# Exp of the last four rows taken row by row in a kernel that sums reciprocals

## The chip, the cores and the metric

One core of a Trainium2 chip. The metric is the device time of one execution in microseconds (us). Engines are named as the profile names them: PE (TensorE), DVE (VectorE), ACT (ScalarE), POOL (GpSimd), SP (SyncE).

## The reference

```python
x = np.abs(np.random.randn(32, 512, 1024)).astype(np.float32) + 1e-6
out = np.sum(1.0 / x, axis=-1)      # 32 x 512 float32
```

Each of the 128 partitions gets 128 rows of 1024 elements: 67 MB to read, 64 KB to write.

## The kernel before

A row is folded in half: 1/a + 1/b = (a + b) / (ab). With the product p = ab, the reciprocal is exp(-ln p), which ACT makes with one Ln and one Exp on half as many elements. There are three kinds of chunk, of two rows each:

- **A**: POOL makes both products. Exp writes the reciprocals rc to PSUM, and DVE sums the whole row (1024 elements) times rc: 1.2 us per row.
- **B**: POOL makes both products. PE adds the halves (a matmul with the identity, accumulated) into s in PSUM; Exp is in place in pr; DVE sums 512 elements of pr times s: 0.68 us per row.
- **C**: like B, but the product of the first row is made by DVE from a copy b of the half row that PE puts into PSUM.

```python
A, B, C = (2, 0, 0), (2, 2, 0), (2, 2, 1)          # rows, rows summed through s, rows whose product DVE makes
LOADS = [[A, B, A, B], [A, B, A, C]] * 5 + [[A, B], [A, C]] * 4 + [[A], [B], [A], [C]] * 2
...
def sum_rows(c, xc, pr, sm, rc):
    m, e = xc.shape[1], len(sm)
    for j in range(e, m):                           # rows of kind A
        row = xc[:, j, :].rearrange("p (h e) -> p h e", h=2)
        sum_row(c + j, row,
                rc[:, j - e, :].unsqueeze(1).to_broadcast([P, 2, H]),
                pr[:, e : e + 2, :] if j == e and m - e > 1 else None)   # where the products go; None: over the row
    for j in reversed(range(e)):                    # rows of kinds B and C, the second one first
        sum_row(c + j, pr[:, j, :], sm[j])
...
        for (m, e, v), pr in zip(chunks, made):     # one chunk
            xc = xt[:, q : q + m, :]
            ...                                     # POOL: products of rows v..m-1 into pr
            sm = []
            for j in range(e):                      # PE: s of row 0, then s of row 1
                s = spool.tile([P, H], f32, tag="s")
                add(s, xc[:, j, :H], xc[:, j, H:])
                sm.append(s)
            if waiting:
                sum_rows(*waiting)                  # DVE: sums of the chunk before
            keep(nc.scalar.activation(out=pr, in_=pr, func=Ln, scale=S))
            rc = None
            if e < m:                               # kind A: one Exp of both rows
                rc = rpool.tile([P, m - e, H], f32, tag="rc")      # rpool has 2 buffers
                i = nc.scalar.activation(out=rc, in_=pr[:, e:, :], func=Exp, scale=-1.0)
                keep(i)
            if e:                                   # kinds B, C: one Exp of both rows
                r = pr[:, :e, :]
                keep(nc.scalar.activation(out=r, in_=r, func=Exp, scale=-1.0))
            waiting = c0 + q, xc, pr, sm, rc
```

The order on every engine is that of the program. The last two chunks are an A (rows 124, 125) and a C (rows 126, 127), each loaded by itself.

## Time and profile before

| | before |
|---|---|
| time, median of 3 | 171.85 us (171.72 to 171.97) |
| span in the profile | 169.9 us |
| PE starts on the last load | 161.10 us |
| last sum's accumulator read starts | 167.06 us |

The last two rows: I call the stretch between them **the tail** (5.96 us here) and what follows to the end of the span **the end phase** (169.94 - 167.06 = 2.88 us: the store and the final barrier). The accumulator read is the instruction that writes a row's finished sum out. Measuring the tail from PE's start takes out the jitter of the loads, which is some tenths of a us. The lines themselves are in the prediction. In a timeline a line has the start and the length in us, the engine, the line of the kernel and the operation, what is written and read, shapes, the count, and in brackets how long the engine had been idle and what released it. L92 is the summing helper on DVE; its form over 1024 elements (ANT_1) is a row of kind A, that over 512 (ANT_0) a row of kind B or C.

### The profile page before, as it was taken

How to read it: one execution, taken by the hardware profiler on the slowest of the kernel's cores; microseconds unless marked ns; L12 is line 12 of the kernel's file. 1: busy time of each engine (PE TensorE's matmuls, PEld its weight loads, DVE VectorE, ACT ScalarE, POOL GpSimd, SP SyncE). 2: the span in 40 equal slices, each digit the busy share in tenths (PEclk: the TensorE clock that was granted, in tenths of full speed). 3: DMA queues.
4: the chain of work that ended last, by engine and by line, in shares of the span. 5: the costliest groups of instructions: out<-in, count | busy, mean ns of one | idle time of the engine just before them, and what ended most of it. 6: DMA issues, size and time to landing. Idle time of an engine off the chain costs nothing.

```text
span 169.9 us, 1267 instructions
## 1 busy us (share of the span) xinstructions
PE 131.7 (77%) x278; PEld 50.5 (30%) x278; DVE 122.3 (72%) x267; ACT 133.9 (79%) x129; POOL 138.3 (81%) x70
## 2 busy tenths in 40 slices
PE   0008999786988789784997869789999999888790
PEld 0003433331332233231432323224334342333230
DVE  0000777767987577767777679778989898889883
ACT  3002989978887987958889787999999988999890
POOL 1008999699996999689996998999999889998920
PEclk9999999999999999999999999999999999999999
DMA  6999999999999999999999999999999999999400
GB/s 208 409 455 409 463 409 455 409 463 401 463 411 447 424 440 420 432 434 424 440 424 440 424 397 434 424 428 426 432 428 432 424 413 417 422 420 424 187 0 15
DMA packets 3894, 67.24 MB, mean 396 GB/s; under 512 B 432, under 2 KB 560, under 8 KB 560
## 3 DMA queue, kind: packets, MB, share of 16 engines
q1 hardware_dynamic: 3888, 67.18, 92.9%
q8 instruction: 2, 0.03, 0.1%
q14 instruction: 4, 0.03, 0.0%
HBM read 67.11 MB, written 0.07 MB: 395 GB/s over the span
## 4 chain that ended last, share of the span: by engine, by line
DMA 78%; POOL 11%; DVE 3%; ACT 2%; issue 2%; SPq 1%; POOLq 0%; DVEq 0%
DMA ring<-in_x_dram 78%; POOL pr L141 11%; DVE pr L92 2%; DVE ring L92 1%; ACT pr L152 1%; ACT rc L156 1%; SPq L122 1%; POOLq L141 0%; DVE sums L92 0%; DVEq L92 0%; DVEq L195 0%
## 5 line engine op out<-in xcount | busy, mean ns | idle before, releaser
L141 POOL TENSOR_TENSOR pr<-ring 128x1024 f32<-128x1024 f32 x64 | 137.6, 2189 | 23.6 <-DMA ring<-in_x_dram 23.3
L82 PE MATMUL s<-ring,ident 128*128 128x512 f32 x256 | 122.4, 616 | 32.5 <-DVE sums L92 16.6
L152 ACT ACTIVATE pr<-pr 128x1024 f32<-128x1024 f32 x64 | 67.4, 1053 | 28.7 <-POOL pr L141 28.5
L82 PEld LDWEIGHTS s<-ring,ident 128*128 128x128 f32 x256 | 47.0, 194 | 105.3 <-issue 63.1
L92 DVE CUSTOM_DVE_ANT_1 pr<-ring,rc 128x1024 f32<-128x1024 f32 x32 | 39.1, 1221 | 44.6 <-ACT rc L156 44.6
L92 DVE CUSTOM_DVE_ANT_0 pr<-pr,s 128x512 f32<-128x512 f32 x64 | 41.3, 683 | 0.2
L92 DVE CUSTOM_DVE_ANT_1 ring<-ring,rc 128x1024 f32<-128x1024 f32 x32 | 38.9, 1216 | 0.0
L162 ACT ACTIVATE pr<-pr 128x1024 f32<-128x1024 f32 x32 | 33.8, 1058 | 1.0
L156 ACT ACTIVATE rc<-pr 128x1024 f32<-128x1024 f32 x32 | 32.9, 1028 | 1.0
L82 PE MATMUL b<-ring,ident 128*128 128x512 f32 x22 | 12.0, 626 | 1.4 <-DMA ring<-in_x_dram 1.4
L92 DVE DVE_READ_ACCUMULATOR2_ANT sums<- 128x1 f32 x128 | 10.6, 83 | 0.0
L130 DVE TENSOR_TENSOR pr<-ring,b 128x512 f32<-128x512 f32 x11 | 7.5, 683 | 0.1
L82 PEld LDWEIGHTS b<-ring,ident 128*128 128x128 f32 x22 | 3.5, 188 | 9.0 <-DMA ring<-in_x_dram 7.6
L53 ACT ACT_TABLE_LOAD x1 | 1.3, 1283 | 0.7 <-PEq L184 0.7
masks.py:197 POOL MEMSET ident<- 128x128 f32 x1 | 0.2, 204 | 0.3 <-POOLq L184 0.3
masks.py:199 POOL TENSOR_SCALAR_AFFINE_SELECT ident<-ident 128x128 f32<-128x128 f32 x1 | 0.3, 292 | 0.1
L184 POOL MEMSET const-float32-0.0<- 128x1 f32 x1 | 0.1, 98 | 0.2 <-issue 0.2
L184 POOL MEMSET const-uint8-127<- 128x1 uint8 x1 | 0.1, 103 | 0.0
L184 POOL MEMSET const-bfloat16-1.0<- 128x1 bf16 x1 | 0.1, 101 | 0.0
L184 POOL MEMSET const-float32-1.0<- 128x1 f32 x1 | 0.1, 98 | 0.0
## 6 DMA issues: line engine op xcount, KB each, us to landing
ring<-in_x_dram SPq DMA_DIRECT2D x10, 4096.0 KB, 37.8
ring<-in_x_dram SPq DMA_DIRECT2D x8, 2048.0 KB, 37.0
ring<-in_x_dram SPq DMA_DIRECT2D x8, 1024.0 KB, 28.3
out_dram<-sums SPq DMA_DIRECT2D x1, 64.0 KB, 1.5
```

The costliest lines, as they stand in the source:

```text
L53: nc.scalar.add_instruction(mybir.InstLoadActFuncSet(name=nc.get_next_instruction_name(), act_func_set_id=act_sets.index("natural_log_exp_ ...
L82: i = nc.tensor.matmul(bank, lhsT=ident, rhs=half, start=k == 0, stop=k == len(halves) - 1,)
L92: i = nc.vector.tensor_tensor_reduce(out=row if out is None else out, in0=row, in1=fac, scale=S, scalar=0.0, op0=mult, op1=plus, accum_out ...
L122: keep(nc.sync.dma_start(out=xt, in_=x_v[:, c0 : c0 + n, :]))
L130: i = nc.vector.tensor_tensor(out=pr[:, j, :], in0=xt[:, q + j, :H], in1=b, op=mult)
L141: i = nc.gpsimd.tensor_tensor(out=pr[:, v:, :], in0=xc[:, v:, :H], in1=xc[:, v:, H:], op=mult)
L152: keep(nc.scalar.activation(out=pr, in_=pr, func=Ln, scale=S))
L156: i = nc.scalar.activation(out=rc, in_=pr[:, e:, :], func=Exp, scale=-1.0)
L162: keep(nc.scalar.activation(out=r, in_=r, func=Exp, scale=-1.0))
L184: nc = _bacc.Bacc("TRN2", target_bir_lowering=False, num_devices=1)
```

## The change

The intent: in the body the loads hide everything, but after the last load nothing does. There the DVE waits for an Exp over two rows although it could start with the first of them. So the last four rows get an Exp of their own each, in the order in which they are summed (124, 125, 127, 126). The first sum of the A chunk writes over its row, as the usual target pr is still read by the second Exp.

```diff
+    SINGLE = 124
@@ sum_rows
-                rc[:, j - e, :].unsqueeze(1).to_broadcast([P, 2, H]),
-                pr[:, e : e + 2, :] if j == e and m - e > 1 else None,
+                rc[j - e].unsqueeze(1).to_broadcast([P, 2, H]),
+                pr[:, e : e + 2, :] if j == e and e + 1 < m and c < SINGLE else None,
@@ after Ln
-            rc = None
-            if e < m:
-                rc = rpool.tile([P, m - e, H], f32, tag="rc")
-                i = nc.scalar.activation(
-                    out=rc, in_=pr[:, e:, :], func=Exp, scale=-1.0
-                )
-                keep(i)
-            if e:
-                r = pr[:, :e, :]
+            step = 1 if c0 + q >= SINGLE else m
+            rc = []
+            for j in range(e, m, step):
+                to = min(j + step, m)
+                r = rpool.tile([P, to - j, H], f32, tag="rc")
+                keep(
+                    nc.scalar.activation(
+                        out=r, in_=pr[:, j:to, :], func=Exp, scale=-1.0
+                    )
+                )
+                rc += [r[:, l, :] for l in range(to - j)]
+            for to in range(e, 0, -step):
+                r = pr[:, max(to - step, 0) : to, :]
                 keep(nc.scalar.activation(out=r, in_=r, func=Exp, scale=-1.0))
```

## The prediction

> **What bounds the kernel now.** I read the page first: busy shares, slices, chain by engine.
>
> ```profile
> PE 131.7 (77%) x278; PEld 50.5 (30%) x278; DVE 122.3 (72%) x267; ACT 133.9 (79%) x129; POOL 138.3 (81%) x70
> ...
> DMA  6999999999999999999999999999999999999400
> ...
> DMA 78%; POOL 11%; DVE 3%; ACT 2%; issue 2%; SPq 1%; POOLq 0%; DVEq 0%
> ```
>
> The transfer engines are full in almost every slice until about 159 us and make 78% of the chain; no compute engine is over 81% busy. So the body runs at the pace of the loads of x, and the change doesn't touch the body: it concerns rows 124 to 127, the last two chunks. Only the tail can move. The busy table by stretches says when the tail begins:
>
> ```profile
> 155.00:161.00 6.00, 4.45 (x10) 1.44 (x8) 5.32 (x13) 5.48 (x6) 5.77 (x3) 1.00 0.69 287
> 161.00:167.20 6.20, 4.56 (x10) 1.82 (x10) 5.54 (x13) 4.12 (x4) 1.42 (x2) 1.00 0.00 0
> ```
>
> The columns are the stretch, its length, then busy time and count of PE, weight loads, DVE, ACT and POOL, the granted clock, the DMA share and GB/s. After 161.0 nothing is loaded. Of the last 6.2 us, DVE works 5.54, PE 4.56 and ACT 4.12. Next the chain of waits in order of time, its last pieces:
>
> ```profile
> 161.17 1.07 ACT pr L152
> 162.24 0.02 issue
> 162.26 1.04 ACT rc L156
> 163.30 0.02 issue
> 163.32 1.22 DVE pr L92
> 164.54 0.01 DVE sums L92
> 164.55 1.13 DVE ring L92
> 165.69 0.01 DVE sums L92
> 165.69 0.01 issue
> 165.70 0.05 DVEq L92
> 165.75 0.09 issue
> 165.84 0.69 DVE pr L92
> ```
>
> This is Ln of rows 124 and 125, their common Exp, the sums of 124 and 125, then the sum of 127 (that of 126 follows, to 167.14). The chain as printed says: shorten the Exp and DVE starts earlier. But between the end of sum 125 and the start of sum 127 stand 0.15 us that an engine with work ready would not spend: a wait instruction of DVE's sequencer (DVEq, 0.05) and 0.09 of issue. So I looked at what else sum 127 needs, in the timelines of PE and DVE:
>
> ```profile
> 161.10 1.13 PE L82 MATMUL b<-ring,ident 128*128 128x512 f32 x2 [1.16 <-DMA ring<-in_x_dram]
> 162.06 3.60 PE L82 MATMUL s<-ring,ident 128*128 128x512 f32 x8
> ```
>
> ```profile
> 162.26 0.69 DVE L130 TENSOR_TENSOR pr<-ring,b 128x512 f32<-128x512 f32 x1
> 163.32 1.22 DVE L92 CUSTOM_DVE_ANT_1 pr<-ring,rc 128x1024 f32<-128x1024 f32 x1 [0.37 <-ACT rc L156]
> ...
> 165.84 0.69 DVE L92 CUSTOM_DVE_ANT_0 pr<-pr,s 128x512 f32<-128x512 f32 x1
> 166.45 0.08 DVE L92 DVE_READ_ACCUMULATOR2_ANT sums<- 128x1 f32 x1
> 166.45 0.68 DVE L92 CUSTOM_DVE_ANT_0 pr<-pr,s 128x512 f32<-128x512 f32 x1
> ```
>
> PE gets the last load at 161.10 (it had waited 1.16 us for it), makes the copy b of row 126's half (two passes), then s of row 126 (four passes) and s of row 127 (four). They start 0.43 us apart, the last at 165.07, and its modelled end is 162.06 + 3.60 = 165.66. Sum 127, which the kernel takes ahead of sum 126, needs exactly the s that is made last. **Two chains meet within 0.03 us:** POOL, ACT and DVE free DVE at 165.69; the last load and ten PE passes make s ready at 165.66. The semaphore records of the trace agree: PE's count rises at 165.673, ScalarE's for the last Exp long before at 165.363, and DVE's wait, which names both, runs at 165.701. The printed chain shows the first chain only.
>
> **What the Trainium skill says.** "ScalarE: Activation LUTs", section "What ACT_TABLE_LOAD costs": an ACTIVATE with immediate scale and bias takes 186 ns and 0.833 ns per element, and back-to-back ones overlap by about 93 ns. For 1024 elements that is 1039 ns; the groups here show 1058 (Exp to SBUF), 1053 (Ln) and 1028 (Exp to PSUM), so it agrees. For 512 elements, which this kernel never has, I take the measured values less 512 x 0.833 = 427 ns: about 0.60 us to PSUM and 0.63 to SBUF. "VectorE: DVE Perf Modes", section "The TRN2 errata — SBUF-src ops pay a fixed extra latency per instruction": an fp32 tensor_tensor takes (N+151)/0.96 ns, 691 at 512 and 1224 at 1024; the sums here take 683 and 1216 to 1221. "Perfetto Trace Analysis", section "Tensor Engine Instruction (MATMUL, LD_WEIGHTS)": the end of a matmul is an estimate of the profiler. Here the copy b ends by that estimate at 161.10 + 1.13 = 162.23 and the DVE product that needs it starts at 162.26, so the estimate is good to some 0.03 us. Same page, section "Identifying Dependency Chains": an instruction that waits on several engines may have an EventSemaphore put before it; the DVEq piece at 165.70 is one.
>
> **The change, part by part.** Nothing is removed; two ACTIVATEs become four.
>
> 1. Exp of rows 124, 125 (1.03 us from 162.26) becomes two of about 0.60. The first ends at 162.26 + 0.60 = 162.86. Sum 124 also stands behind the DVE product of row 126, 162.26 to about 162.91 (such a product passes DVE on after 0.65: 153.50 to 154.15 earlier in the timeline). So sum 124 starts near 162.91, not 163.32: **0.41 us earlier**.
>
> 2. The second Exp starts 0.60 less the overlap of 0.06 later (here Exp to the next Ln is 0.97 from start to start for 1.03 of duration): 162.80, done at 163.40. Sum 124 lasts until 162.91 + 1.15 = 164.06, so sum 125 doesn't wait. It frees DVE at 165.69 - 0.41 = 165.28.
>
> 3. Each rc tile now holds one row and there are two buffers, so row 125 takes the buffer of rows 120 and 121. Their sums were done at 160.83, 1.9 us before it is asked for: no cost.
>
> 4. Sum 124 writes over its row in ring rather than into pr, so that it doesn't wait for the second Exp, which reads pr. Means of both forms: 1221 and 1216 ns. No cost.
>
> 5. Ln of rows 126, 127 starts at about 162.80 + 0.54 = 163.34 instead of 163.23, **0.11 later**, the fixed part of one more ACTIVATE. Exp of 127 then runs 164.41 to 165.04, that of 126 from 164.94 to 165.57. Before, the common Exp ended at 165.36. So ScalarE has row 127 ready 0.32 us earlier and row 126 0.21 later, but sum 126 isn't due before 166.45.
>
> 6. Sum 127 needs DVE (165.28), Exp of 127 (165.04) and s of 127 (165.66, unchanged: PE's passes hang on the load that landed at 161.1 and on nothing that the change moves). It starts after the last of these and the same wait: 165.66 + 0.04 + 0.14 = 165.84, **as before**. Both last sums then follow back to back, end at 167.14, and the store (1.5 us to landing) follows unchanged.
>
> Sum: 0.41 us won on DVE at sum 124, 0.41 us spent again in front of sum 127; about 0.00, at most some hundredths. From 171.85: **171.80 us**, as in some executions the load may come a little earlier against POOL's chain and leave PE less late.
>
> **The rivals.** First, *the whole 0.41 us arrives*: PE's ends are modelled and the printed chain names no PE at all, so s might be ready earlier than it seems. Then sum 127 starts near 165.43 and the time is 171.85 - 0.41 = 171.44. Against it stand the PE semaphore at 165.673 and the unexplained gap of 0.15. Second, *the split costs time*: two more fixed parts of about 0.11 us each on ScalarE. If Exp of 126 ended after 166.45 it would count; by step 5 it has 0.88 us to spare. If the wait tracking made sum 127 wait for both Exp (they write one tile), it would wait until 165.60, still before PE. So at most 0.1, or 171.95. Third, *the loads decide*: a program whose body is bound by transfers shows nothing of a change in the tail; here the tail after the last load is 6 us of compute, so this is no reason by itself, but the last landing fixes PE's chain, and a landing some tenths earlier or later against POOL's chain gives any gain from 0 to 0.41.
>
> **Range and chances.** Runs of the kernel before spread over 171.72 to 171.97. With about 0.7 for PE's wait (171.75 to 171.9), 0.2 for part or all of the 0.41 (171.44 to 171.7) and 0.1 for a small loss, I say 171.80 us, 171.50 to 172.05. 2% is 3.4 us, more than half of the whole tail: faster 0.01, within 2% 0.98, slower 0.01.
>
> **What would show it.** Exp over 512 elements in the tail at about 0.60 us (PSUM) and 0.63 (SBUF); sum 124 about 0.4 us sooner after Ln of its chunk; sum 125 directly behind it; then a gap of DVE of about 0.55 us before sum 127, put down to PE or to DVE's sequencer; and a printed chain whose end now goes through PE and the last load instead of POOL and ACT. I am wrong if the gap isn't there and sum 127 follows sum 125 within 0.2 us (then the gain is near 0.4), if Exp takes clearly over 0.65 us, or if a wait for the rc buffer stands before the second Exp.

## More of the kernel before

Ratios are with executions of the kernel before on the same chip and in the same rounds; the rounds ran on several chips, on which the kernel before took 171.71 to 171.83 us (medians), so differences of a tenth of a us between rounds are taken from the kernel before, not from the times alone.

## The result, and the profile after

The changed kernel took 171.97 us (median of 4, 171.89 to 172.06), the kernel before 171.83 in the same rounds. The ratio is 1.0008, with a 95% interval of 0.999 to 1.0025: no difference that these runs can tell from none. (A ratio is the mean time of one kernel's fast runs over that of the other's of the same rounds, so not quite the ratio of the medians.)

First ACT in the timeline of the changed kernel: the two split Exp, with Ln of the last chunk between them.

```profile
162.31 1.12 ACT L161 ACTIVATE r<-pr 128x512 f32<-128x512 f32 x2
163.37 1.04 ACT L153 ACTIVATE pr<-pr 128x1024 f32<-128x1024 f32 x1
164.44 1.15 ACT L168 ACTIVATE pr<-pr 128x512 f32<-128x512 f32 x2
```

The four took 602 and 583 ns to PSUM and 630 and 612 ns to SBUF in the trace. Then DVE's timeline:

```profile
162.32 0.69 DVE L131 TENSOR_TENSOR pr<-ring,b 128x512 f32<-128x512 f32 x1
163.04 1.22 DVE L93 CUSTOM_DVE_ANT_1 ring<-ring,r 128x1024 f32<-128x1024 f32 x1
...
164.19 1.22 DVE L93 CUSTOM_DVE_ANT_1 ring<-ring,r 128x1024 f32<-128x1024 f32 x1
165.33 0.08 DVE L93 DVE_READ_ACCUMULATOR2_ANT sums<- 128x1 f32 x1
165.87 0.69 DVE L93 CUSTOM_DVE_ANT_0 pr<-pr,s 128x512 f32<-128x512 f32 x1 [0.46 <-PE s L83]
...
167.09 0.08 DVE L93 DVE_READ_ACCUMULATOR2_ANT sums<- 128x1 f32 x1
```

Sum 124 starts 1.88 us after PE's start on the last load (163.04 - 161.16) instead of 2.22 (163.32 - 161.10): 0.34 us gained. Sum 125 is done 0.34 us earlier too. But sum 127 starts at 4.71 instead of 4.74, because DVE now stands idle for 0.46 us, and the view names the engine it waits for: PE, s. The last accumulator read comes at 5.93 instead of 5.96. The gain of 0.34 us has become a wait. The chain of waits of the changed kernel now says so as well:

```profile
141.38 19.74 DMA ring<-in_x_dram
...
161.16 1.13 PE b L83 x2
162.29 3.45 PE s L83 x8
165.74 0.03 issue
165.76 0.02 DVEq L93
165.78 0.09 issue
165.87 0.11 DVE pr L93
```

Where the chain of before went through POOL, ACT and DVE, this one goes from the last load through ten passes on PE to sum 127. PE's chain was there before the change too. It was even the last by 0.06 us: PE's count (the semaphore that tells DVE that s is done) rose at 165.67, and DVE could have gone on at 165.61, as e3 below shows. It was not printed because the view takes DVE to be busy until the accumulator read ends.

### The profile page after: what moved, and what is told of

The parts are those of the page before. It is cut to its first block, busy times and chain, and to the rows that moved or that the text cites. A ratio compares the mean times of both kernels' runs of the same rounds, so it can differ in the third digit from the quotient of the medians.

```text
span 170.1 us, 1269 instructions
## 1 busy us (share of the span) xinstructions
PE 132.4 (78%) x278; PEld 50.8 (30%) x278; DVE 122.4 (72%) x267; ACT 134.1 (79%) x131; POOL 138.3 (81%) x70
## 4 chain that ended last, share of the span: by engine, by line
DMA 79%; POOL 7%; issue 3%; PE 3%; ACT 3%; DVE 2%; SPq 1%; DVEq 0%; POOLq 0%
DMA ring<-in_x_dram 79%; POOL pr L142 7%; PE s L83 2%; ACT pr L153 2%; DVE ring L93 1%; SPq L123 1%; DVE pr L93 1%; PE b L83 1%; ACT r L161 1%; DVEq L201 0%; ACT pr L168 0%; DVE sums L93 0%; POOLq L142 0%; DVEq L93 0%
## 5 line engine op out<-in xcount | busy, mean ns | idle before, releaser
L153 ACT ACTIVATE pr<-pr 128x1024 f32<-128x1024 f32 x64 | 67.4, 1053 | 28.7 <-POOL pr L142 28.6
L93 DVE CUSTOM_DVE_ANT_1 pr<-ring,r 128x1024 f32<-128x1024 f32 x31 | 37.9, 1221 | 43.8 <-ACT r L161 43.8
L93 DVE CUSTOM_DVE_ANT_1 ring<-ring,r 128x1024 f32<-128x1024 f32 x33 | 40.1, 1216 | 0.0
L168 ACT ACTIVATE pr<-pr 128x1024 f32<-128x1024 f32 (+1 forms) x33 | 33.9, 1031 | 1.0
L161 ACT ACTIVATE r<-pr 128x1024 f32<-128x1024 f32 (+1 forms) x33 | 33.0, 1002 | 1.0
L83 PE MATMUL b<-ring,ident 128*128 128x512 f32 x22 | 12.8, 667 | 1.5 <-DMA ring<-in_x_dram 1.4
```

Of the source, the lines that this page charges most:

```text
L83: i = nc.tensor.matmul(bank, lhsT=ident, rhs=half, start=k == 0, stop=k == len(halves) - 1,)
L93: i = nc.vector.tensor_tensor_reduce(out=row if out is None else out, in0=row, in1=fac, scale=S, scalar=0.0, op0=mult, op1=plus, accum_out ...
L161: nc.scalar.activation(out=r, in_=pr[:, j:to, :], func=Exp, scale=-1.0)
```

## The experiments

Twelve runs were made, all with correct results and with five rounds each (e11 and e12 list six executions). The theory: PE's s of row 127, made last and needed first, holds sum 127 back and takes the gain (the PE theory). The rivals: the added ACTIVATEs and waits eat a real gain; or PE's modelled ends mislead and PE has nothing to do with it. This table holds the readings for all runs; the tail and the end phase are worked out from each trace as above.

| run | PE on last load, us | tail, us | end phase, us | time, us | ratio to before (95%) |
|---|---|---|---|---|---|
| before | 161.10 | 5.96 | 2.88 | 171.85 | |
| after | 161.16 | 5.93 | 3.02 | 171.97 | 1.0008 (0.999 to 1.0025) |
| e1, after again | 161.30 | 5.93 | 3.01 | 171.85 | 1.0003 (0.9991 to 1.0016) |
| e2, after, s exchanged | 161.18 | 5.37 | 2.95 | 171.32 | 0.997 (0.9958 to 0.9983) |
| e3, before, s exchanged | 161.21 | 5.70 | 3.01 | 171.69 | 0.9994 (0.9982 to 1.0007) |
| e4, after, PE delayed | 161.61 | 6.79 | 3.02 | 172.85 | 1.0057 (1.0043 to 1.0071) |
| e5, before, PE delayed | 161.23 | 6.82 | 2.88 | 172.68 | 1.0049 (1.0037 to 1.0061) |
| e6, e2 with A split only | 161.12 | 5.66 | 3.02 | 171.54 | 0.9989 (0.9975 to 1.0003) |
| e7, e2 with C split only | 161.25 | 5.70 | 2.95 | 171.79 | 1.0005 (0.9992 to 1.0017) |
| e8, e2, first sum to pr | 161.15 | 5.80 | 2.95 | 171.57 | 0.9996 (0.9983 to 1.0009) |
| e9, after, last chunk B | 161.22 | 5.40 | 2.72 | 171.10 | 0.9963 (0.9951 to 0.9976) |
| e10, before + 1 DVE instruction | 161.35 | 5.96 | 3.09 | 172.14 | 1.0016 (1.0003 to 1.0028) |
| e11, after + 24 | 162.16 | 7.63 | 2.71 | 173.44 | 1.0092 (1.0055 to 1.0129) |
| e12, e2 + 24 | 162.16 | 5.31 | 2.65 | 171.96 | 1.0037 (1.0004 to 1.007) |

The kernel before, in the rounds of e1 to e4, took 171.78 us (median of 9), in those of e6 to e9 171.71, and in those of e5 and e10 to e12 171.77.

### e1: the changed kernel again

> The changed kernel once more, for an interval on the same chip as the next three. The tail is measured in each trace from the start of PE's first pass over the last load to the start of the last accumulator read: 5.96 us before the change (161.10 to 167.06), 5.93 after it (161.16 to 167.09). PE theory (the wait for s of row 127 took the 0.41 us): the same time as before to 0.1 us, ratio 0.999 to 1.001, tail 5.90 to 5.96. Rival (ScalarE's and the waits' added costs ate a real gain, so the change does harm): ratio 1.001 to 1.002.

Measured: 171.85 against 171.78, ratio 1.0003, tail 5.93. As the PE theory has it. Two sets of rounds now hold the change within 0.3% of nothing.

### e2 and e3: s of row 127 ahead of s of row 126

Both have the same edit, e2 on the changed kernel, e3 on the kernel before:

```diff
-            sm = []
-            for j in range(e):
+            sm = [None] * e
+            for j in reversed(range(e)) if c0 + q == F - 2 else range(e):
                 s = spool.tile([P, H], f32, tag="s")
                 add(s, xc[:, j, :H], xc[:, j, H:])
-                sm.append(s)
+                sm[j] = s
```

> The changed kernel, with s of row 127 made on PE ahead of s of row 126 in the last chunk, so that the sum taken first has its s 1.7 us earlier. PE theory: the gap before sum 127 shrinks from 0.46 us to 0.15 or less, the tail falls from 5.93 to between 5.47 and 5.62, the time is 0.3 to 0.45 us below the changed kernel's (ratio to before 0.997 to 0.9985). Rival (PE's modelled ends mislead; the added ACTIVATEs or waits set the end): tail 5.9, no change of time.

> The kernel before, with the same exchange of the two s on PE and nothing else. PE theory with both chains level: DVE is free at 4.59 us after PE's start (165.69 - 161.10), so only the wait instruction is saved: tail 5.82 to 5.94, 0.02 to 0.14 us less. Rival (PE's order alone is worth all that the run with both has, the split is worth nothing): tail about 5.5, as in the run with both.

DVE's timeline of e2, from the end of sum 125 on:

```profile
165.33 0.08 DVE L93 DVE_READ_ACCUMULATOR2_ANT sums<- 128x1 f32 x1
165.33 0.68 DVE L93 CUSTOM_DVE_ANT_0 pr<-pr,s 128x512 f32<-128x512 f32 x1
```

The gap is gone: sum 127 starts in the same moment as the accumulator read of sum 125. The tail is 5.37, 0.56 us less than with the change alone, and the time is 0.53 us less than e1 in the same rounds. Both are more than I had expected (5.47 to 5.62, and 0.3 to 0.45 us): a miss in size, for the same reason as in e3. No instruction was taken away. So the split did make room, and PE's order filled it. The rivals, which had no change here, fall.

In e3 it is the same, from the end of sum 125 on:

```profile
165.69 0.08 DVE L92 DVE_READ_ACCUMULATOR2_ANT sums<- 128x1 f32 x1
165.69 0.68 DVE L92 CUSTOM_DVE_ANT_0 pr<-pr,s 128x512 f32<-128x512 f32 x1
```

The tail of e3 is 5.70, 0.26 us less than before. I had expected 0.02 to 0.14: a miss in the useful direction. The reason is in the lines above. DVE hands on to the next sum when the accumulator read starts, not when it ends, so before the change it could have gone on at 165.61 rather than 165.69; and a wait that is already met costs nothing, while one that has to be sat out costs its wait instruction and 0.09 us of issue. PE cost the kernel before not 0.1 but 0.23 us (4.51 to 4.74 us after PE's start) in front of sum 127; the other 0.03 us of the 0.26 are a chain through POOL that in e3 starts that much earlier after PE's start (Ln of rows 124 and 125 at 0.04 us instead of 0.07). In time, e3 and before can't be told apart (0.9994), for a reason that comes up below: its end phase is 0.13 us longer. With PE's order exchanged, the split is worth 5.70 - 5.37 = 0.33 us of the tail; without, 0.03.

### e4 and e5: PE delayed on purpose

Two needless passes ahead of s of row 127, whose result is written over:

```diff
                 s = spool.tile([P, H], f32, tag="s")
+                if c0 + q + j == F - 1:
+                    add(s, xc[:, j, :H])
                 add(s, xc[:, j, :H], xc[:, j, H:])
```

> The changed kernel with two needless passes of 0.43 us on PE just ahead of s of row 127 (written, then written over; the result stays right). PE theory: everything behind moves by the whole 0.86 us: tail 6.79, the time up by 0.8 to 0.9 us (ratio to before about 1.005). Rival (PE is not what sum 127 waits for): the delay is hidden at least in part, under 0.5 us.

> The kernel before with the two needless passes on PE just ahead of s of row 127. If PE was already the last to be ready for sum 127 before the change (it cost 0.23 to 0.26 us there by the run with the exchange alone), the whole 0.86 us shows: tail 6.82, time up by 0.8 to 0.9 us; then the two kernels end alike, 6.82 and 6.79. If VectorE was what sum 127 waited for before the change, part of the delay is hidden: tail under 6.7.

The tails are 6.79 and 6.82, as expected to the hundredth: the whole 0.86 us shows in both, although in the kernel before the printed chain named no PE. In the timeline of e5 the wait has the right name, too:

```profile
165.73 0.08 DVE L92 DVE_READ_ACCUMULATOR2_ANT sums<- 128x1 f32 x1
166.83 0.69 DVE L92 CUSTOM_DVE_ANT_0 pr<-pr,s 128x512 f32<-128x512 f32 x1 [1.01 <-PE s L82]
```

The times rose by 1.00 us over e1 and 0.91 over before; e4's excess over 0.86 is not in the tail (its last load came 0.3 us later than e1's in the profiled executions) and within the interval.

### e6, e7, e8: which part of the change does it, once PE is out of the way

All three have e2's exchange. e6 splits rows 124 and 125 only, e7 rows 126 and 127 only, e8 lets the first sum write to pr again:

```diff
-            step = 1 if c0 + q >= SINGLE else m          # e6
+            step = 1 if c0 + q == SINGLE else m
-    SINGLE = 124                                         # e7
+    SINGLE = 126
-  ... if j == e and e + 1 < m and c < SINGLE else None,  # e8
+  ... if j == e and e + 1 < m else None,
```

> As the run with the exchanged s after the change (tail 5.37), but rows 126 and 127 get one common Exp again; only rows 124 and 125 are split. DVE is free for sum 127 at 4.15 us from PE's start as there; the common Exp runs from 3.26 to 4.32 and is seen at 4.35. So sum 127 starts at 4.35 to 4.45 and the tail is 5.57 to 5.67: 0.2 to 0.3 us lost of the 0.33 that the split is worth once PE's order is exchanged (5.70 without any split). Rival (the first split alone makes the gain): tail 5.4.

> The other half: exchanged s, only rows 126 and 127 split, rows 124 and 125 with a common Exp and the first sum written to pr as before the change. DVE is bound to sums 124 and 125 until 4.48 whatever Exp of 127 does, so the tail is that of the exchange without a split, 5.70 (5.65 to 5.75). Rival (each split is worth its own part): about 5.5.

> Exchanged s and both splits, but the sum of row 124 is again written to pr, which Exp of row 125 still has to read. Sum 124 must then wait for that Exp, done at 2.25 us from PE's start: it starts at 2.28 to 2.38 rather than 1.86, and the tail is 5.79 to 5.90, worse than 5.70 without any split. Rival (the target of the first sum is indifferent, as its duration is the same): tail 5.37.

Tails 5.66, 5.70 and 5.80, each within what was expected (the times agree less well: by tail and end phase together, e6, e7 and e8 should be 0.15, 0.19 and 0.09 us below the kernel before; measured against its 171.71 they are 0.17 below, 0.08 above and 0.14 below. e7's profiled execution, 171.67, was the fastest of its five. All three intervals include no change). Measured from e3's 5.70 without any split, the first split alone is worth 0.04 us, the second alone 0.00, and both 0.33. They are links of one chain: the first frees DVE earlier, and then sum 127 finds no Exp unless that is split too. In DVE's timeline of e6 that is this gap:

```profile
165.26 0.08 DVE L93 DVE_READ_ACCUMULATOR2_ANT sums<- 128x1 f32 x1
165.56 0.69 DVE L93 CUSTOM_DVE_ANT_0 pr<-pr,s 128x512 f32<-128x512 f32 x1 [0.22 <-issue]
```

The view gives it to "issue"; the common Exp of rows 126 and 127, which runs from 164.37 to 165.43 in ACT's timeline of e6, is what ends just ahead of the sum. In e8 the gap is in front of sum 124 and is named:

```profile
163.44 1.22 DVE L93 CUSTOM_DVE_ANT_1 pr<-ring,r 128x1024 f32<-128x1024 f32 x1 [0.44 <-ACT r L161]
```

The sum waits for an Exp whose result it doesn't use, because it wants to write where that Exp still reads. So the small edit of the target is not decoration: without it the split makes the tail longer (5.80) than no split at all (5.70).

### e9: PE's wait taken away in another way

```diff
+    LOADS[-1] = [B]
```

POOL makes both products of the last chunk; PE makes no copy b, DVE no product.

> PE's wait taken away in another way: the changed kernel in its own order of s, but in the last chunk GpSimd makes both products, so PE makes no copy b (two passes of 0.43 us fewer) and DVE no product. PE is done with s of 127 at 3.7 us from its start on the last load. GpSimd takes 2.37 rather than 1.28 us, so Ln of the last chunk starts at 2.53 instead of 2.21, Exp of 127 ends at 4.23 and sum 127 starts at 4.26 to 4.4: tail 5.45 to 5.6, against 5.93. If PE were not what the changed kernel waits for, this would cost time (Ln 0.3 us later): tail over 5.93.

The tail is 5.40, slightly under the range, and the time 171.10, the lowest of all. Lines of PE and DVE in its timeline:

```profile
161.22 3.67 PE L85 MATMUL s<-ring,ident 128*128 128x512 f32 x8 [1.25 <-DMA ring<-in_x_dram]
```

```profile
165.28 0.08 DVE L95 DVE_READ_ACCUMULATOR2_ANT sums<- 128x1 f32 x1
165.40 0.69 DVE L95 CUSTOM_DVE_ANT_0 pr<-pr,s 128x512 f32<-128x512 f32 x1
```

PE is done at 161.22 + 3.67 = 164.89, 0.5 us before sum 127, with its order of s unchanged. Ln of the last chunk starts 0.22 us later after PE's start than in the changed kernel (2.43 against 2.21); that doesn't undo it. Two independent ways of taking PE out of the path gain 0.53 and 0.56 us of the tail, where the theory without PE had a longer tail for e9; that settles the PE theory. (That the two gains are alike is chance: sum 127 of e9 starts behind its Exp, 0.12 us after DVE is free.)

### e10, e11, e12: the end phase

The table has a second column that moves. The end phase grew from 2.88 to 3.02 us with the change, and e9, with nearly the tail of e2, is 0.22 us faster (0.15 when each is taken from the kernel before of its own rounds); its end phase is 2.72, 0.23 us shorter than that of e2. In the view of what SP's queue waited for, the kernel before and the changed one differ in this line:

```profile
SPq L195 <- PEq L195: 0.6, 2, 0.4
```

```profile
SPq L201 <- PEq L201: 0.9, 2, 0.7
```

It is the final barrier, and the view names PE; the records of single instructions name another. After the last accumulator read, DVE's drain (an instruction of the barrier) comes at 2.38 us before and at 2.67 after the change. In every trace up to e9 with at least 320 DVE instructions the 320th comes late. Before the change that is the very last record, on which nothing waits (it ends the span 0.08 us after the last record of any other engine); the change adds one wait instruction on DVE, and now it is the drain in front of the barrier. e9 has 318 and no late one (the expectation of e10 says ten traces, which wrongly counts e9). To test the count itself I added DVE instructions that do nothing of use:

```diff
+    pad = opool.tile([P, n], f32)             # n = 1 in e10, 24 in e11 and e12
+    for k in range(n):
+        keep(nc.vector.memset(pad[:, k : k + 1], 0.0))
```

> In all ten traces the 320th instruction record of VectorE comes 0.1 to 0.5 us late; before the change that is its very last record, after the change (one wait instruction more) the one before, the end barrier's drain, and the end phase from the last accumulator read to the end of the span grows from 2.88 to 3.02 us. Here: the kernel before, plus one VectorE instruction (it clears one element per partition of an unused tile, at the start, where VectorE idles). Count theory: 321 records, the drain late again, end phase 2.95 to 3.05 instead of 2.88, tail as before the change (5.96); time up by about 0.1 us. Rival (the longer end phase belongs to the changed order of work, or is chance): end phase 2.88.

> The changed kernel plus 24 such VectorE instructions at the start. Count theory: the 320th record now falls among the sums of rows 114 to 118, where the delay is hidden behind the loads or absent, the end phase is 2.72 as in the run with 318 records, tail 5.93, time 0.2 to 0.35 us below the changed kernel's (ratio to before 0.998 to 0.9995). Rival: end phase 3.02 and no gain, or another late record at the end.

> The changed kernel with the exchanged s on PE and the 24 instructions: tail 5.37, end phase 2.65 to 2.72; time 0.23 us below the exchange alone, 171.05 to 171.15, ratio to before about 0.996, the fastest of all. Rival (count theory wrong): as the exchange alone, ratio 0.997.

e10 supports the count: same tail as before (5.96), end phase 3.09, a little over the range, time 171.77 to 172.14. One idle instruction costs 0.2 us at the very end. (The change itself shows only 0.14 of it, as in it SP sits out one of its final waits, some 0.08 us, under the store.) The rest of the 0.37 us is in the loads and noise: PE starts on the last one 0.25 us later in the profiled execution. The timeline of e10 has a by-catch. In front of sum 127 is the same gap as in the kernel before (0.25 us from the accumulator read, 0.23 there), and in this trace the view names what it had left out there:

```profile
166.09 0.69 DVE L95 CUSTOM_DVE_ANT_0 pr<-pr,s 128x512 f32<-128x512 f32 x1 [0.17 <-PE s L85]
```

In e11 and e12 the end phase fell to 2.71 and 2.65, as expected, and yet both are **slower**: I was wrong on the time. What I hadn't counted on stands in PE's timeline, e12 first, then e11:

```profile
162.16 1.13 PE L86 MATMUL b<-ring,ident 128*128 128x512 f32 x2 [2.14 <-DMA ring<-in_x_dram]
163.12 3.60 PE L86 MATMUL s<-ring,ident 128*128 128x512 f32 x8
```

```profile
162.16 1.54 PE L86 MATMUL b<-ring,ident 128*128 128x512 f32 x2 [2.18 <-DMA ring<-in_x_dram]
163.50 4.92 PE L86 MATMUL s<-ring,ident 128*128 128x512 f32 x8
```

The last load came 1 us late. The view of the transfers between 159.0 and 162.2 us has this in e12 (and the same line in e11), and no such line in e2:

```profile
q14 instruction: 1, 0.01, 0.6%
```

A block of 8 KB of instructions was fetched, at 160.4 us. In e2 the like of it comes at 169.8, beside the end; the fetch that e2 has at 117.2 comes at 100.7 in e12. Only DVE's program differs between the two, by 24 instructions, so these fetches are DVE's, and the padding moved one into the last load.

The records of single packets, which the view adds up, show how the two meet. In e12 one transfer engine's packets of 8 KB follow each other 0.31 us apart up to 160.07; the fetch is the next in that row, at 160.38; behind it comes the row's last packet of the load, at 160.69, which takes 0.97 us instead of 0.31. One landing of the load comes at 162.11, its other fifteen by 160.53. In e11 the fetch, at 160.63, stands in such a row too, with only the packet of 4 bytes behind it that tells of the landing; one landing comes at 162.12, the others by 161.09. (The records don't name the engine; that a row is one engine's is read from its even spacing.) So the late landing is that of the engine that made the fetch. Why it comes 1 us late, when the fetch itself takes 0.32 us, stays open, and no run moved the fetch alone.

In e11's profiled execution the granted clock is 0.50 from 162.74 to 166.15 us, and PE after its 2.18 us of waiting ran its next passes 0.85 us apart instead of 0.43, so that sum 127 waited 1.86 us for s. e11's times fall into two groups, 172.52 to 172.63 and 174.25 to 174.27, and e12's into 171.89 to 171.96 and 173.50 to 173.56; the half pace is seen in e11's trace (of the later group), not in e12's (of the earlier). Of e11, the three executions of the later group have a mean granted clock of 0.98, the other three of 1.00. So the medians of these two runs are of mixed groups, and their ratios say no more than "slower".

### The better version

e2 and e9 beat both kernels, by 0.3% and 0.37%, with intervals clear of 1. e9 is a single line on top of the change. Its lead over e2 is within the two intervals, and in the traces lies in the end phase (2.72 against 2.95), which goes with DVE's instruction count, so that another edit can take it away.

## Why the prediction was right

By its own steps:

1. *Sum 124 starts 0.41 us earlier.* Mis-sized: 0.34. Exp was sized right (602 ns for an estimate of 0.60), but the product of row 126 was taken to hand DVE on after 0.65 us as where nothing is waited for. Sum 124 has to sit out a wait: Exp's count rose at 162.926, and the sum, behind a wait instruction of its own, began 0.12 us later. (Before the change the sum itself waited and began 0.02 us after the count, 163.300 to 163.323.)
2. *Sum 125 doesn't wait.* Right: 164.19 is the moment of the accumulator read of sum 124.
3. *The rc buffer costs nothing.* Right: the two Exp start 0.54 us apart, without a wait between.
4. *The other target costs nothing.* Right for the duration (1221 and 1216 ns), and e8 showed what the old target would have cost.
5. *Ln of the last chunk 0.11 us later, Exp of 126 harmless.* Right: Ln at 2.21 us after PE's start instead of 2.13, the Exp of 126 over at 165.59, sum 126 starts at 166.49. This is the rival of added costs on ACT, and e2 leaves nothing of it in the tail.
6. *Sum 127 starts when it did, after PE's s.* Right, and the core of it: 4.71 against 4.74; moved by e2 and e9, and by e4 with the full 0.86 us.

Of the rivals, the full gain of 0.41 us didn't arrive; e2 against e3 shows that 0.33 us of it were there to be had. The third rival, a load that lands earlier or later against POOL's chain, didn't come into play: Ln of rows 124 and 125 starts 0.06 to 0.07 us after PE in the kernel before, in the changed kernel and in e1. The two chains were not level within 0.03 us, with DVE the last: PE was the last by 0.06, and cost the kernel before 0.23 us (e3). Step 6 came out right all the same, as it took over the measured wait of the kernel before. And its last clause, that what follows the last sum is unchanged, failed: the end phase grew by 0.14 us. In sum, -0.03 in the tail and +0.14 after it, and 0.07 to 0.14 us more measured, within the noise of the rounds. The time, 171.97, is inside the full range given, but above the 171.75 to 171.9 that the prediction gave to PE's wait alone, and on the other side of the kernel before than its 171.80: no step foresaw the end phase, and the small gain hoped for from the loads didn't come.

## What to carry to other kernels

A printed chain shows only the chain that ended last: before shortening a link, look up everything else that the next instruction waits for, above all where a small gap has no cause; here a chain that the profile didn't print was within 0.06 us and took nine tenths of the gain. Work that is consumed in one order should be produced in that order on every engine that feeds it: exchanging two groups of matmuls made the same split worth ten times as much of the tail (0.33 us instead of 0.03). And differences of a tenth of a per cent are read in the trace from a fixed event, not from the total, as the end of this program had costs of its own that moved with most of the edits.

## What the Trainium skill lacked or had wrong

- "Perfetto Trace Analysis", section "Identifying Dependency Chains", names the EventSemaphore put ahead of an instruction that waits on several engines, but no cost. Here it costs nothing when its counts are met in time (sum 127 of e2 starts with the accumulator read before it), and 0.12 to 0.17 us from the count to the start of the sum when it has to be sat out (PE: 165.67 to 165.84 before, 165.74 to 165.87 after; Exp: 162.93 to 163.04 after). A sum that waits by itself starts 0.02 us after the count (163.300 to 163.323 before).
- The fetch of an engine's instructions has a place in "Runtime: NRT & Kernel Launch", section "Instruction fetch mechanics", which calls the cost of going from one block to the next mostly hidden; it has no case in which it isn't. In e11 and e12 a fetch of 8 KB at 160.6 and 160.4 us stands in the packets of one transfer engine just ahead of the end of the last load, and that engine's landing comes 1 us late.
- No page was found that has a certain instruction of an engine's program come late: the 320th of DVE, by some 0.1 to 0.4 us in the eleven traces that had it in the final barrier, worth 0.2 us of the end phase in e10. What makes it late stays open. That it begins a new block of instructions is a guess; it would fit that the three fetches that move with DVE's program began when DVE had started 62, 197 and 321 records in e2, and 69, 188 and 323 in e12, about 128 apart. No run tests it.
- "TensorE: Matmul & The Clock Gate", section "What's actually happening", says that PE falls to half its clock after an idle window of about 3.4 us, and that the windows run free. The length agrees: the half clock of e11 lasts 3.41 us. But the window need not be idle throughout: the 3.41 us before it held 1.23 us of PE work and 2.18 us of waiting. e12's wait of 2.14 us lies across two such windows, 1.07 us on each, and no half clock follows. Nor is e11 alone: the clock records of the changed kernel and of e2, e3, e4, e6, e7 and e10 have one half-clock stretch of 3.41 us each between 60 and 86 us, e11 a second one there, each after 1.9 to 2.3 us of idle PE in the 3.41 us before; 2.02 us in the kernel before brought none. There the loads set the pace.
